# Grouping the output products of the RWKV head pairs by kind instead of by chunk

## The chip, the cores and the metric

The kernel runs on one core of a Trainium2 chip. The metric is device time in microseconds (us), from launch to the end of the program. Engines are named as in the profile: PE is TensorE (matrix products), PEld its weight loads, DVE is VectorE, ACT is ScalarE, POOL is GpSimd, SP is SyncE, which issues the transfers.

## The reference

Two blocks of a model work on 512 tokens with 1024 features. The first has two layers, each a feed-forward part, a mixer and a second feed-forward part. The mixer runs six RWKV heads, six heads of dilated attention and a convolution side by side. Each RWKV head keeps a 64x64 state and steps it over the tokens:

```
state = state * w_t + sa * b_t + v_t * k_t      # sa = state a_t
y_t   = state r_t
...
y = ((y - mean(y)) * rsqrt(var(y) + eps)) * ln_w + ln_b
out = (y + bonus) * g
```

The second block (gated linear attention, sparse attention, convolutional feed-forward parts) follows and is not touched.

## The kernel before

The two heads of a pair lie side by side: head 0 on partitions 0 to 63 (`hb[0]`), head 1 on 64 to 127 (`hb[1]`). There are three pairs a layer and two layers, six pairs in all. `rwkv_pair` cuts the 512 tokens into 8 chunks of 64. For each chunk the output is a sum of two products, collected in one bank of PSUM (`pY`, [128, 8, 64]): scores by values, `SR[h][:, n]` by `VV[h][:, n]`, with 128 rows of contraction and 64 columns; and from the second chunk on queries by the state at the chunk's start, `Rt` by `S`, with 64 rows and 64 columns. That is 16 score products and 14 state products a pair, 30 together, 180 in the program. A float32 product of this kind shows as two MATMUL records in the trace.

The states come from a loop of seven steps before (L683 on PE, L684 on DVE). Behind the output products stand a group norm (L695 to L705: sums on DVE, a square on ACT, Newton steps of `rsqrt` at L300 to L305, a product on POOL), transposes back to features by tokens (L711, copied by ACT), the gate (L715) and two DVE operations (L716, L717) that finish `out[i]`.

Order: the mixer's parts are traced by turns (`MIXER`), and a scheduler ranks them, so on each engine the instructions of the three pairs (PSUM banks `rr`, `rz`, `rx`), of the attention (banks `at`, `po`), and of `mem_kv` (bank `mm`, operands `mh`, `ml`) are interleaved. Each engine then runs its list strictly in order. `mem_kv` multiplies eight weight blocks, each in 24 MATMULs of 256 columns at L270 to L272. Then `out_proj` runs twice over eight blocks of 12 MATMULs: the first time over pairs `rr` and `rz` and the convolution, the second time over attention and pair `rx`. Each weight block is split into a high part by ACT (L258, `whi`) and a low part by DVE (L259, `wlo`), with two buffers each.

Of the kernel before, what the change touches and what calls it, by code (L numbers as in the profile page):

```python
# [18 lines left out]
T = 512  # L19
# [18 lines left out]
# ---------------------------------------------------------------- constants that depend on shapes alone  # L38

def const_pack():  # L40
    """Small tables side by side, [128, n], and where each begins."""
# [26 lines left out]
def dil_table():  # L68
    """ALiBi and pattern multiplicity of the dilated attention, [head, p, u], key minus query = u - 384 - p."""
    p = np.arange(128)[:, None]  # L70
    u = np.arange(512)[None, :]
    d = p + 384 - u
    m = (d <= 128) * 1.0 + (d % 4 == 0) + (d % 16 == 0)
    m = np.where(d >= 0, m, 0.0)
    with np.errstate(divide="ignore"):
        lm = np.log(m)
    out = [np.where(m > 0, -s * d + np.where(m > 0, lm, 0.0), NEG) for s in SLOPES_6]
    return np.ascontiguousarray(np.stack(out).astype(np.float32))
# [9 lines left out]
def nsa_table():  # L88
    """ALiBi of the causal heads, [head, p, u], u as above."""
    p = np.arange(128)[:, None]  # L90
    u = np.arange(512)[None, :]
    d = p + 384 - u
    return np.ascontiguousarray(np.stack([np.where(d >= 0, -s * d, NEG) for s in SLOPES_8]).astype(np.float32))


def cmp_tables():
    """Bias [2, p, 2, head, 32] of the tokens' tiles over compressed blocks, and which count [p, 4, 32]."""
# [9 lines left out]
def gla_masks():  # L107
    """[2, p, 512]: by levels, keys p in the first half and queries in the second half of one block."""
# [13 lines left out]
# ---------------------------------------------------------------- layout of the inputs  # L122

def pack_w(w):
    """[K, N] to [N/128, 128, K]: the 128x128 tiles of each block of 128 columns side by side."""
# [4 lines left out]
class Vecs:  # L130
    """Vectors over features as columns of 128."""
# [14 lines left out]
# ---------------------------------------------------------------- the program  # L146
# [4 lines left out]
# where the hidden units of the feed-forward parts lie  # L151
HIDDEN = ["r0"] * 8 + ["r1"] * 8 + ["aq"] * 3 + ["ap"] * 3

# the order of the mixer's parts, by turns
# [13 lines left out]
class Part:  # L168
    """A part of the program that is traced by turns, and where its tiles come from. The scheduler takes its first turn
    in the order of the program, the later ones by the part's rank from a place in the program on."""  # L170
# [16 lines left out]
class Net:  # L187
# [21 lines left out]
    def on(self, heap, bank, lane=""):  # L209
        """Where tiles come from until the next call."""  # L210
        self.heap, self.bank, self.lane = heap, bank, lane

    def drive(self, parts, plan):
        """Traces parts of the program by turns; the plan names parts, with the number of turns."""
# [5 lines left out]
    def rank(self, base, n):  # L220
        """The scheduler's rank of what is traced next, counted from a place in the program: low ones go first."""
        self.tc.cur_priority = base + RANK * n
# [17 lines left out]
    def s(self, shape, tag="s", dt=F32, heap=None):  # L240
        """A tile of at most 2 KB a partition from a heap."""
# [8 lines left out]
    # ------------------------------------------------ products of float32 in three passes  # L250

    def load_w(self, dram, cols):
        """One chunk of weights: DMA, then its high and low parts (exact: hi + lo is the weight to 24 bits)."""
# [8 lines left out]
    def gemm(self, ps, w, xs, k0, k1, first, last):  # L262
        """ps (+)= W^T X over the k-tiles k0..k1 of the chunk; xs gives (hi, lo) of a k-tile."""
# [10 lines left out]
    def proj(self, dram, xs, n=T):  # L274
        """One block of 128 outputs over 1024 inputs, left in PSUM."""
# [5 lines left out]
    def split(self, src, scale=None, heap=None):  # L281
        """(hi, lo) of a tile, times a constant; src may lie in PSUM."""
# [11 lines left out]
    # ------------------------------------------------ norms  # L294

    def rsqrt(self, x, shape, tag="rs", iters=3):
        """1/sqrt(x) of positive x by Newton's steps."""
# [10 lines left out]
    def bcast(self, r, q, heap=None, bank=None):  # L308
        """[128 tok, q] to [128, q*128], the same on every partition."""
# [11 lines left out]
    def norm_r(self, x, nt=T):  # L321
        """The tokens' 1/rms over 1024 features, the same on every partition."""
# [16 lines left out]
    def scaled(self, x, gname, l0=0, nt=T, heap=None):  # L339
        """(hi, lo) of x*g, tile by tile."""  # L340
# [10 lines left out]
    # ------------------------------------------------ feed-forward parts  # L351
# [50 lines left out]
    def out_proj(self, x, w, m, k0=0, k1=KT, bank="mm"):  # L402
        """x += W^T m over the k-tiles k0..k1; m their (hi, lo)."""
# [5 lines left out]
    def spill(self, x):  # L409
        """Parks x in DRAM; the function that it returns brings it back."""  # L410
# [14 lines left out]
    # ------------------------------------------------ helpers of the mixers  # L425

    def to_tok(self, src, to=None):
        """[128 ch, 512 tok] to [128 tok, 4, 128 ch]."""
# [9 lines left out]
    def head_sums(self, ps, c0, src):  # L438
        """Sums over each of two heads' 64 channels: ps[tok, j, c0:c0+2]."""
# [3 lines left out]
    def head_bcast(self, r, heap=None):  # L443
        """r [128 tok, 4, 2] to PSUM [128 ch, 512], each head's number over its 64 channels."""
# [7 lines left out]
    def derived(self):  # L452
        """Vectors worked out once: 1 - mu, 1 - k_a, halves of biases, the product of the heads' gains."""
# [16 lines left out]
    # ------------------------------------------------ RWKV  # L470

    def shifted(self, l, blk, win, xs, R):
        """A projection with its token shift, p + (prev - p) mu, in features by tokens."""
# [8 lines left out]
    def rwkv_shared(self, l, win, xs, R):  # L482
        """What the low-rank parts read: tanh of the decays', the rates', sigmoid of the gates'; and their weights."""
# [10 lines left out]
    def rwkv_pair(self, l, i, win, xs, R, shared, out):  # L494
        """Two heads, by chunks of 64 tokens; out gets the result in features by tokens.

        Within a chunk f_t = r_t + sum_{s<t} N[s, t] f_s is solved with D, the inverse of the diagonal blocks of 16, and
        M = (N without these) D, whose fourth power is zero: f = D (r + M (r + M (r + M r))). Rows are (head, token in
        its chunk); of head 0 the scores' rows are the keys of b, then those of k, of head 1 the other way round."""
# [9 lines left out]
        # decay, rate  # L509
# [21 lines left out]
        # keys  # L531
# [32 lines left out]
        # scores, keys by queries: a's columns before the token, r's up to it  # L564
# [13 lines left out]
        # the diagonal blocks, a block in a partition, and their inverses  # L578
# [7 lines left out]
        # tokens by channels  # L586
# [75 lines left out]
        # the state's step over a chunk: S' = ec (G^T S + H), [j, i] of each head; the first state is zero  # L662
# [23 lines left out]
        # outputs, and the norm of each head's group  # L686
        pY = self.ps([128, 8, 64])
        for n in range(8):
            for h in range(2):
                self.T.matmul(pY[hb[h], n], SR[h][:, n], VV[h][:, n], start=True, stop=True)  # L690
                if n:
                    self.T.matmul(pY[hb[h], n], Rt[hb[h], 64 * n:64 * n + 64], S[hb[h], n], start=False, stop=True, skip_group_check=True)
# [27 lines left out]
    # ------------------------------------------------ attention  # L720

    def softmax(self, ps, bias, n, z, heap=None):
        """exp(ps + bias - max) by rows; z gets the rows' sums."""
# [10 lines left out]
    def causal_pair(self, score, V, tables, z, po, heap):  # L734
        """Causal attention of two heads, four tiles of queries each: po[head's channel, t] without the division by z.
        score(ps, h, i) leaves a tile's products with the keys up to its end; V(h, b) gives a block of a head's values."""
# [32 lines left out]
    def dilated_pair(self, l, i, win, xs, R, out):  # L769
        """The dilated attention of two heads: one softmax over all keys, each as often as patterns hold it."""  # L770
# [38 lines left out]
    # ------------------------------------------------ convolution  # L809
# [82 lines left out]
    # ------------------------------------------------ attention to the memory  # L892

    def mem_kv(self, l):
        """Keys [dh, m] and values [m, dh] of the memory's four heads, to DRAM."""
# [52 lines left out]
    def mem_attend(self, heads, mq, kv, out, c0=4):  # L948
        """Some of the four heads' results, (hi, lo) by features and tokens."""
# [44 lines left out]
    # ------------------------------------------------ gated linear attention  # L994

    def gla_pair(self, i, win, xs, R, low, mk, Vk, rr, out):
        """Two heads over all tokens. A query and an earlier key share, on one level of halving, a block whose
        middle lies between them; their decay is the product of the two parts up to the middle, both at most 1."""
# [125 lines left out]
    # ------------------------------------------------ sparse attention  # L1124

    def twice(self, f, g, n=T, heap=None):
        """The high and the low parts of half of a tile, each on both halves of the partitions. Against queries whose
        parts lie on the halves, two passes give the product of float32."""
# [8 lines left out]
    def windows(self, kc, which):  # L1137
        """The compressed blocks' halves, by the parity of the token and the channel, with their positions added."""
# [11 lines left out]
    def hidden(self, ph):  # L1150
        """Hidden units of the compressed blocks, [128 units, 2, keys and values, 2 groups, 32]; the 32nd block is none."""
# [17 lines left out]
    def compressed(self, kc, vc, q, gates, C):  # L1169
        """The compressed blocks' part, to C[pair][channel of two heads, t]."""  # L1170
# [85 lines left out]
    def stream_pair(self, u, st, q, K, V, gates, O, bank):  # L1256
        """Causal attention of two heads over all tokens' keys and values, to O, the second onto the first: all blocks (eight are selected of
        eight), or the window, which holds all tokens."""
# [143 lines left out]
# ---------------------------------------------------------------- the launch  # L1402

def pack_first(a):
    """The first block's inputs as the program reads them."""
# [105 lines left out]
```

## Time and profile before

| | us |
|---|---|
| runs of the kernel: lowest, median, highest | 3510.12, 3514.63, 3515.13 |
| profiled execution: first to last instruction (span) | 3510.5 |
| PE busy in the span | 3465.2 |
| DVE, ACT, POOL busy | 1749.7, 1229.8, 538.4 |
| score products of all pairs (L690), first to last start | 661.3 to 1832.9 |

The profiled execution has only its span; the median run is 4.1 us longer. Engines work at once, so their busy times overlap. PE is busy in nearly all of the span, but a busy PE is not PE at its peak.

### The profile page before, as it was taken

The numbers are of one execution on the slowest core, as the hardware profiler recorded it, in microseconds if no ns is written. First come the engines' busy times: TensorE is split into PE (matmuls) and PEld (weight loads), VectorE is DVE, ScalarE is ACT, GpSimd is POOL, SyncE is SP. The second block draws the span as 40 slices with busy tenths as digits, with TensorE's granted clock in tenths as the row PEclk, the third lists the DMA queues.
The fourth block names the chain that finished last, engine by engine and source line by source line (L and its number), as shares of the span: only waits on it lengthen the run. The fifth ranks groups of instructions, "written<-read, shape, count | busy, mean of one in ns | idle before, by whom it ended". The sixth has DMA issues, their size and how long they took to land.

```text
span 3510.5 us, 43279 instructions
## 1 busy us (share of the span) xinstructions
PE 3465.2 (99%) x17126; PEld 2763.0 (79%) x17126; DVE 1749.7 (50%) x2857; ACT 1229.8 (35%) x1946; POOL 538.4 (15%) x509
## 2 busy tenths in 40 slices
PE   8999999999999999999999999999999999999998
PEld 6888777778888888877777888777888887778886
DVE  4433498454333443359755333385655354455532
ACT  3222334343222222233434222244433234643332
POOL 2110024011111111012401111120111000211100
PEclk9999999999999999999989999999999999999999
DMA  3223322132223222332214223321322333122232
GB/s 137 91 95 108 100 78 64 34 116 92 96 92 95 95 91 93 112 98 77 53 39 137 96 96 99 112 79 63 106 91 95 105 123 102 49 92 95 92 96 79
DMA packets 127594, 321.55 MB, mean 92 GB/s; under 512 B 32385, under 2 KB 34977, under 8 KB 127393
## 3 DMA queue, kind: packets, MB, share of 16 engines
q1 hardware_dynamic: 127392, 318.80, 28.6%
q8 instruction: 134, 2.20, 0.3%
q14 instruction: 68, 0.55, 0.1%
HBM read 303.81 MB, written 14.94 MB: 91 GB/s over the span
## 4 chain that ended last, share of the span: by engine, by line
PE 94%; DVE 3%; POOL 1%; issue 1%; ACT 0%; DMA 0%; SPq 0%; DVEq 0%; POOLq 0%; ACTq 0%
PE mm L272 13%; PE mm L270 12%; PE mm L271 12%; PE at L270 8%; PE at L271 8%; PE at L272 8%; PE rr L272 4%; PE rr L270 4%; PE rr L271 4%; PE rx L270 3%; PE rx L272 3%; PE rx L271 3%; PE po L748 1%; PE at L798 1%; POOL Z L616 1%
## 5 line engine op out<-in xcount | busy, mean ns | idle before, releaser
L258 ACT ACTIVATE whi<-raw 128x1024 fp32r<-128x1024 f32 (+2 forms) x566 | 562.1, 994 | 1680.9 <-issue 529.6
L259 DVE TENSOR_TENSOR wlo<-raw,whi 128x1024 fp32r<-128x1024 f32 (+2 forms) x566 | 651.2, 1151 | 505.8 <-ACT whi L258 491.0
L270 PE MATMUL mm<-xh,whi 128*128 128x512 f32 x1216 | 486.4, 400 | 9.7 <-ACT whi L258 9.7
L272 PE MATMUL mm<-xh,wlo 128*128 128x512 f32 x1216 | 487.8, 401 | 0.0
L271 PE MATMUL mm<-xl,whi 128*128 128x512 f32 x1216 | 485.1, 399 | 0.7 <-DVE xl L347 0.7
L270 PE MATMUL at<-xh,whi 128*128 128x512 f32 x736 | 291.7, 396 | 0.0
L272 PE MATMUL at<-xh,wlo 128*128 128x512 f32 x736 | 291.0, 395 | 0.0
L271 PE MATMUL at<-xl,whi 128*128 128x512 f32 x736 | 290.8, 395 | 0.0
L270 PEld LDWEIGHTS mm<-xh,whi 128*128 128x128 f32 x1216 | 229.3, 189 | 65.6 <-ACT whi L258 10.1
L373 POOL TENSOR_TENSOR fg<-fg,bR 128x512 f32<-128x512 f32 x88 | 155.3, 1767 | 806.5 <-ACT fg L372 806.5
L272 PEld LDWEIGHTS mm<-xh,wlo 128*128 128x128 f32 x1216 | 229.0, 188 | 61.3 <-issue 3.9
L271 PEld LDWEIGHTS mm<-xl,whi 128*128 128x128 f32 x1216 | 229.1, 188 | 57.3 <-issue 2.5
L270 PE MATMUL mm<-hi,whi 128*128 128x512 f32 x652 | 259.5, 399 | 2.4 <-ACT hi L287 1.5
L272 PE MATMUL mm<-hi,wlo 128*128 128x512 f32 x652 | 257.6, 396 | 0.0
L271 PE MATMUL mm<-lo,whi 128*128 128x512 f32 x652 | 257.4, 395 | 0.1
L331 POOL TENSOR_TENSOR nacc<-nacc,nsq 128x512 f32<-128x512 f32 x70 | 107.0, 1528 | 772.7 <-ACT nsq L330 772.2
L272 PEld LDWEIGHTS at<-xh,wlo 128*128 128x128 f32 x736 | 138.1, 188 | 36.1 <-DVE wl L514 1.5
L271 PEld LDWEIGHTS at<-xl,whi 128*128 128x128 f32 x736 | 138.2, 188 | 34.5 <-issue 1.5
L272 PE MATMUL rr<-xh,wlo 128*128 128x512 f32 x416 | 164.4, 395 | 0.8 <-DVE wlo L259 0.8
L270 PEld LDWEIGHTS at<-xh,whi 128*128 128x128 f32 x736 | 138.2, 188 | 33.8 <-ACT gy L1004 0.8
L270 PE MATMUL rr<-xh,whi 128*128 128x512 f32 x416 | 164.6, 396 | 0.0
L271 PE MATMUL rr<-xl,whi 128*128 128x512 f32 x416 | 164.3, 395 | 0.0
(667 smaller groups left out, 5975.1 us busy)
## 6 DMA issues: line engine op xcount, KB each, us to landing
raw<-ffn_gu SPq DMA_DIRECT2D x176, 512.0 KB
raw<-c_gu SPq DMA_DIRECT2D x88, 512.0 KB
raw<-ffn_dn SPq DMA_DIRECT2D x64, 448.0 KB
raw<-w_in SPq DMA_DIRECT2D x46, 512.0 KB
raw<-ffn_dn SPq DMA_DIRECT2D x32, 512.0 KB
raw<-c_dn SPq DMA_DIRECT2D x32, 448.0 KB
raw<-a_w_in SPq DMA_DIRECT2D x17, 512.0 KB
park<-x SPq DMA_DIRECT2D x32, 256.0 KB
```

The source lines that it names most:

```text
L258: self.A.activation(hi, raw, AF.Copy)
L259: self.V.tensor_tensor(lo, raw, hi.bitcast(F32), OP.subtract)
L270: self.T.matmul(ps, wh, xh, start=first and j == 0, stop=False)
L271: self.T.matmul(ps, wh, xl, start=False, stop=False)
L272: self.T.matmul(ps, wl, xh, start=False, stop=last and j == nk - 1)
L331: self.G.tensor_tensor(acc, acc, sq, OP.add)
L373: self.G.tensor_tensor(g, g, R, OP.mult)
L616: self.G.tensor_tensor(Z[:, 0, 0:t, t:16], Z[:, 0, 0:t, t:16], tmp[:, 0:t, 0:nt], OP.add)
L748: self.T.matmul(po[64 * h:64 * h + 64, i * 128:(i + 1) * 128], V(h, b), PT[h][:, b * 128:(b + 1) * 128], start=b == 0, stop=b == i)
L798: self.T.matmul(ps, q[b, i * 128:(i + 1) * 128], k[b, 0:(i + 1) * 128], start=True, stop=True)
```

## The change

All 16 score products of a pair are issued first, then all 14 state products. The first score product of each head now marks the bank as fresh (`start=n == 0`) where every score product did so before; the other products add to the bank. Operands, shapes and number of products stay. The two loops take one more line, so every line below stands one further down (L692 becomes L693, L711 becomes L712). Comments and docstrings were emptied too.

```
         pY = self.ps([128, 8, 64])
         for n in range(8):
             for h in range(2):
-                self.T.matmul(pY[hb[h], n], SR[h][:, n], VV[h][:, n], start=True, stop=True)
-                if n:
-                    self.T.matmul(pY[hb[h], n], Rt[hb[h], 64 * n:64 * n + 64], S[hb[h], n], start=False, stop=True, skip_group_check=True)
+                self.T.matmul(pY[hb[h], n], SR[h][:, n], VV[h][:, n], start=n == 0, stop=True, skip_group_check=True)
+        for n in range(1, 8):
+            for h in range(2):
+                self.T.matmul(pY[hb[h], n], Rt[hb[h], 64 * n:64 * n + 64], S[hb[h], n], start=False, stop=True, skip_group_check=True)
```

The scheduler makes a new order of it. On PE, the output products of the last pair (`rx`) of the first layer stood like this before, a score product and a state product of one head, then of the other:

```order
L690 MATMUL rx_4921<-VV_4357,SR_4271 64x64
L690 MATMUL rx_4921<-VV_4358,SR_4272 64x64
L690 MATMUL rx_4921<-VV_4357,SR_4271 64x64
L692 MATMUL rx_4921<-rS_4815,Rt_4156 64x64
L690 MATMUL rx_4921<-VV_4358,SR_4272 64x64
L692 MATMUL rx_4921<-rS_4815,Rt_4156 64x64
L690 MATMUL rx_4921<-VV_4357,SR_4271 64x64
L692 MATMUL rx_4921<-rS_4815,Rt_4156 64x64
```

Now they stand in two blocks, the heads in turns in each (the last score products and what follows them):

```order
L690 MATMUL rx_4921<-VV_4357,SR_4271 64x64
L690 MATMUL rx_4921<-VV_4358,SR_4272 64x64
L690 MATMUL rx_4921<-VV_4357,SR_4271 64x64
L690 MATMUL rx_4921<-VV_4358,SR_4272 64x64
L693 MATMUL rx_4921<-rS_4815,Rt_4156 64x64 x14
L712 MATMUL rr_4801<-cpack,gn_y_4717 64x128 x4
L938 MATMUL mm_5662<-cpack,mvf_5660 128x128 x2
```

In the first pair (`rr`) other work still cuts into the two blocks at six places, in the second (`rz`) at three.

The second place is PE at the start of `out_proj`. Before, the last `mem_kv` block is followed by its transposes (L937) and by whole blocks of `out_proj` (`mm_5817`), and the transposes of pair `rx` (L711) come 24 products later:

```order
L272 MATMUL mm_5752<-mh_5459,wlo_5749 128x256
L937 MATMUL mm_5779<-cpack,mvf_5777 128x128 x2
L270 MATMUL mm_5817<-hi_5801,whi_5820 128x512
L271 MATMUL mm_5817<-lo_5802,whi_5820 128x512
L272 MATMUL mm_5817<-hi_5801,wlo_5821 128x512
L270 MATMUL mm_5817<-hi_5805,whi_5820 128x512
```

Now the first four transposes of `rx` stand ahead of `out_proj`, the other four and the gate (L716) inside its first two blocks (`mm_5817`, `mm_5837`), which run in turns:

```order
L272 MATMUL mm_5752<-mh_5459,wlo_5749 128x256
L712 MATMUL rx_4977<-cpack,gn_y_4955 64x128 x4
L938 MATMUL mm_5779<-cpack,mvf_5777 128x128 x2
L270 MATMUL mm_5817<-hi_5801,whi_5820 128x512
L271 MATMUL mm_5817<-lo_5802,whi_5820 128x512
L272 MATMUL mm_5817<-hi_5801,wlo_5821 128x512
L270 MATMUL mm_5817<-hi_5805,whi_5820 128x512
L712 MATMUL rx_4984<-cpack,gn_y_4955 64x128 x4
L270 MATMUL mm_5837<-hi_5801,whi_5840 128x512
L271 MATMUL mm_5837<-lo_5802,whi_5840 128x512
```

The third place is DVE between the first sum of pair `rx` and the last Newton step of its `rsqrt`, 31 instructions now. It begins so:

```order
L696 TENSOR_REDUCE gn_m_4952<-rx_4921 128x8
L305 SCALAR_TENSOR_TENSOR gn_r_4882<-gn_r_t_4883,gn_r_4882 128x8
L697 TENSOR_SCALAR gn_m_4952<-gn_m_4952 128x8
L303 TENSOR_TENSOR gn_r_t_4883<-gn_r_4882 128x8
L699 TENSOR_TENSOR gn_y_4955<-rx_4921,gn_m_4952 128x512
L304 SCALAR_TENSOR_TENSOR gn_r_t_4883<-gn_r_t_4883,gn_v_4879 128x8
L717 SCALAR_TENSOR_TENSOR bv_3662<-yf_4793,vec,bv_3662 128x512
```

The Newton steps of pair `rz` (`gn_r_4882`) now lie between those of `rx`; before they were over when `rx` began. The second layer's order changes in the same way. POOL's order stays; a few transfers on SP change places.

## Rows read from the trace of the kernel before

**Rows 1.** The page: PE's busy time, and the chain that ended last, by engine.

```profile
PE 3465.2 (99%) x17126; PEld 2763.0 (79%) x17126; DVE 1749.7 (50%) x2857; ACT 1229.8 (35%) x1946; POOL 538.4 (15%) x509
...
PE 94%; DVE 3%; POOL 1%; issue 1%; ACT 0%; DMA 0%; SPq 0%; DVEq 0%; POOLq 0%; ACTq 0%
```

**Rows 2.** Chain of waits, 640 to 800 and 1780 to 1900 us: shares by line.

```profile
by line: PE mm L272 17.1%; PE mm L270 16.8%; PE mm L271 16.4%; PE at L798 3.9%; PE po L748 3.1%; PE rz L692 2.9%; PE rx L690 2.9%; PE rz L690 2.8%; PE rx L692 2.8%; PE rr L690 2.4%; PE rr L692 2.1%; PE at L742 2.1%; PE rr L272 1.2%; PE at L
by line: PE mm L272 19.0%; PE mm L270 18.6%; PE mm L271 17.9%; PE rz L692 3.9%; PE rx L690 3.7%; PE rx L692 3.7%; PE rz L690 3.7%; PE po L748 3.5%; PE rr L690 3.2%; PE rr L692 2.8%; PE at L742 2.8%; PE at L798 2.4%; PE rx L676 1.6%; PE rx L
```

**Rows 3.** Chain of waits, longest pieces: start, us taken, line and MATMUL records.

```profile
654.14 0.61 PE rx L672 x16
655.71 0.73 PE rr L676 x20
662.01 0.26 PE rr L690 x2
692.68 1.90 PE rx L676 x32
703.48 0.40 PE rx L690 x2
716.14 1.05 PE rr L715 x2
717.19 0.56 PE rz L711 x4
```

**Rows 4.** Windows cut where the granted clock is low: busy us (instructions), clock, DMA.

```profile
668.59:672.00 3.41, 3.41 (x35) 2.85 (x35) 0.63 (x5) 0.99 (x4) 0.00 (x0) 0.50 0.00 0
682.25:695.90 13.65, 13.65 (x91) 10.65 (x92) 4.43 (x15) 1.23 (x2) 0.00 (x0) 0.50 0.09 34
702.73:712.97 10.24, 10.24 (x50) 8.44 (x51) 2.71 (x5) 2.57 (x5) 0.00 (x0) 0.50 0.01 2
1808.65:1822.30 13.65, 13.65 (x91) 10.78 (x92) 4.79 (x19) 1.23 (x2) 0.00 (x0) 0.50 0.08 31
1829.13:1835.95 6.82, 6.82 (x35) 5.42 (x35) 1.56 (x3) 0.75 (x2) 0.00 (x0) 0.50 0.00 0
```

**Rows 5.** Chain of waits in the last four of these windows: shares by line.

```profile
by line: PE rz L692 25.2%; PE rz L690 23.9%; PE rx L676 13.9%; PE mm L272 8.4%; PE mm L270 8.4%; PE at L449 7.7%; PE mm L271 6.2%; PE po L748 3.7%; PE rx L683 3.0%
by line: PE rx L692 23.7%; PE rx L690 23.2%; PE rr L711 18.0%; PE mm L272 10.4%; PE rz L711 8.3%; PE mm L270 8.3%; PE mm L271 8.3%
by line: PE rz L692 24.9%; PE rz L690 21.4%; PE rx L676 13.9%; PE mm L270 10.0%; PE mm L272 10.0%; PE at L449 7.7%; PE mm L271 6.2%; PE po L748 3.7%; PE rx L683 3.0%
by line: PE rx L692 35.5%; PE rx L690 30.4%; PE rr L711 14.5%; PE mm L272 9.3%; PE mm L270 6.2%; PE mm L271 6.2%
```

**Rows 6.** Timeline of PE, first layer, end of `mem_kv`: start, us, instruction [idle before].

```profile
708.73 0.41 PE L271 MATMUL mm<-ml,whi 128*128 128x256 f32 x1
708.94 0.41 PE L272 MATMUL mm<-mh,wlo 128*128 128x256 f32 x1
...
713.01 0.37 PE L270 MATMUL mm<-mh,whi 128*128 128x256 f32 x1
...
716.07 1.12 PE L715 MATMUL rr<-lora_u,lora_w 64*128 64x512 f32 x2
...
725.76 0.41 PE L937 MATMUL mm<-cpack,mvf 128*128 128x128 f32 x2 [0.61 <-ACT whi L258]
```

**Rows 7.** Timeline of DVE in the same stretch: start, us, instruction [idle before].

```profile
707.55 0.69 DVE L695 TENSOR_REDUCE gn_m<-rx 128x8 f32<-128x512 f32 x1 [6.09 <-PE rx L692]
...
717.89 1.22 DVE L259 TENSOR_TENSOR wlo<-raw,whi 128x1024 fp32r<-128x1024 f32 x1
...
723.14 0.17 DVE L304 SCALAR_TENSOR_TENSOR gn_r_t<-gn_r_t,gn_v 128x8 f32<-128x8 f32 x1
...
729.00 0.69 DVE L407 TENSOR_TENSOR x<-mm,x 128x512 f32<-128x512 f32 x1 [2.11 <-PE mm L272]
```

**Rows 8.** Timeline of POOL: the product that ends the group norm of pair `rx`.

```profile
726.45 1.34 POOL L705 TENSOR_TENSOR gn_y<-gn_y,gn_r 128x512 f32<-128x512 f32 x1 [23.78 <-DVE gn_r L305]
```

## Prediction

> **What bounds the kernel now.** I read the page first: PE is busy for 99% of the span, and 94% of the chain that ended last lies on PE [rows 1]. So the question for any change is whether it takes time from PE, and whether PE then has to wait for something that it has hidden so far. Next I asked the chain of waits for the two stretches in which the output products run, the end of the mixer in each layer. In 640 to 800 us the six shares at L690 and L692 (pairs rr, rz, rx) add up to 15.9% of 160 us, 25.4 us; in 1780 to 1900 us they add up to 21.0% of 120 us, 25.2 us [rows 2]. Together 50.6 us for 180 products, 0.28 us each, and all of it lies on the chain. Elsewhere in the program nothing of the change is executed.
>
> The third view is the list of pieces of that chain [rows 3]. A group of two records is one product. In turns by kind, one takes 0.26 us at the full clock (662.01) and 0.40 us at the low one (703.48). Work of the same shape that stands in one kind costs much less. L672 is a product of 128 rows by 64 columns into the same kind of bank, the heads in turns, added to later by state products, which is the shape of a score product: 16 records take 0.61 us, 0.076 us a product. L676 has the shape of a state product, 64 by 64: 20 records take 0.73 us, 0.073 us a product. So about 0.18 us of the 0.26 us is not arithmetic; it appears when a product of 128 rows and one of 64 rows alternate, and when the two heads do not follow each other within one kind.
>
> The fourth view is the granted clock. [...] The chain in the four long ones gives the output products 49.1% of 13.65, 46.9% of 10.24, 46.3% of 13.65 and 65.9% of 6.82 us, 22.3 us in sum [rows 5]; at these lines the chain spends more than anywhere else in each. Other work takes the remaining 25.5 us of the 47.8.
>
> **What the change removes.** A pair's 30 products stand in two blocks now. Priced by the neighbours of like shape at the full clock, 180 x 0.076 = 13.7 us. Work of other shapes still cuts in at nine places in a layer, and each of the three pairs changes from one kind to the other once. For each of these 12 I take 0.1 us, between nothing and the 0.18 us above, since much of the other work that cuts in has the shape of one of the two kinds: 2.4 us for both layers. That is 16.1 us against 50.6: **34.5 us saved**. Bounds: at the low clock the like work costs 1.90 us for 32 records (692.68), 0.119 us a product, so 21.4 + 2.4 us, and only 27 us are saved; with no cost at the cuts 37 us.
>
> [...] Score products of both heads use all 128 rows; only their columns differ. In the row the 16 records of L672 do follow each other in 0.61 us [rows 3]. [...]
>
> **The clock.** The low level comes in stretches in which products in turns are the largest item [rows 5]. The stretch before them, with blocks of L672 and L676 at 654 to 656 us, has small products too and runs at the full rate by its own prices [rows 3]. I therefore take it that the low level goes where the turns go. The products' share of this is in the 34.5 us already. For the other 25.5 us: a memory product takes 0.21 us in the low stretch (708.73 to 708.94), and 24 take 3.06 us at the full clock (713.01 to 716.07), 0.128 us each [rows 6]. So 25.5 x (1 - 0.128 / 0.21) = **10.0 us saved**. Bounds: nothing, if the low stretches stay, and 12.8 us if all of it halves.
>
> [...]
>
> **What it adds: waits at the end of the mixer.** Before, PE was so slow that everything else was early: its wait at the last transposes was 0.61 us [rows 6]. Now PE comes to `out_proj` some 20 us sooner in each layer, but VectorE has the same work to do. Two places matter.
>
> First, the transposes of pair rx (L712) stand ahead of `out_proj` now, where they stood two blocks later. PE's queue can't pass them, and they need the group norm of rx. DVE's queue from the first sum to the last Newton step has 31 instructions: 17 small ones at 0.17 us, 13 of at most 0.69 us, one split of a weight block of 1.22 us [rows 7], 13.1 us, and then POOL's product, 1.34 us [rows 8]: 14.4 us. PE meanwhile has three memory blocks of 3.06 us [rows 6], three groups of four transposes at about 0.56 us and two gates at 1.05 us [rows 3], 13.0 us. PE waits about 1.4 us, and everything in `out_proj` behind it.
>
> Second, the first two blocks of `out_proj` run in turns and end together. So the next two weight blocks are split only after both: two additions into x and a split, three DVE instructions of 0.69 us [rows 7], about 2.1 us, of which four products of PE cover about 1.0. Another 1.1 us. Together 2.5 us a layer, **5 us lost**. Bounds: nothing, if the handoffs overlap better than this, and 10 us a layer, if DVE's queue is held up at each of its own waits for PE and ACT, as the 6.09 and 2.11 us idle times in its rows now are [rows 7]. Transfers are no candidate: in the low windows the sixteen DMA engines are busy for 0.09 of the time or less [rows 4].
>
> **Sum.** -34.5 - 10.0 + 5 = -39.5 us, against the profiled span of 3510.5 us 3471.0. The median of the runs is 4.1 us above this span, and I keep that distance: 3514.6 - 39.5 = **3475 us**.
>
> **The rivals.**
> *The clock stays low* (chance 0.14): the low level is a matter of small products and not of turns. For: the low windows hold L676 too. Against: the stretch at 654 us. Then 27 + 0 - 2.5 (PE is slower, so less waiting) = 24.5 us, 3490.
> *No new waits* (0.13): 44.5 us, 3470.
> *DVE's queue binds* (0.14): waits of 10 us a layer, 24.5 us, 3490. For: in the 31 instructions rz's Newton steps now lie between those of rx. Against: of the 20.2 us that the same chain takes now (707.55 to the end of POOL's product at 727.79), 3 us and more are idle.
> *Score products don't pair* (0.04): 39.5 - 17 = 22.5 us, 3492.
> *The change doesn't do what it says* (0.02): the 0.18 us belongs to adding into a bank just written, not to the alternation. For: the added state product follows its own score product now. Against: L683's loop adds in the same way. Then nothing is saved, 3515.
> *Slower* (0.02): the last chain stands alone. If the transposes ahead of `out_proj` had to wait out the whole norm of rx, 20.2 us a layer, and the two blocks in turns were held up by 5 us more by their second transposes, that were 50 us against 44.5 saved: 3520. It decides from 22 us of wait a layer; the 13 us of PE work between speak against it.
>
> **How the numbers follow.** The forecast has 0.51, and its own range is 3468 to 3483. The range for 8 in 10 has to take in the clock and the queue cases: 3462 to 3492; below 3462 both savings would have to be at their upper bound with no wait, 37 + 12.8 = 49.8 us. About 0.2%, 7 us, can be told from no change. Faster by more than that holds in all cases but the last two: 0.95; within it 0.03; slower 0.02.
>
> **What would show it.** In the profile after: records at L690 in blocks with about 0.04 us each, and the shares of L690 and L693 in the two stretches at 7 to 9 us a layer instead of 25; a granted clock of 1.00 where four windows read 0.50; a wait of PE before the first transposes of rx (L712) and at the third block of `out_proj`, of one to three us each, ended by POOL, DVE or ACT. I would be wrong if the records at L690 stayed at 0.1 us and more, if the low windows stayed, or if PE's idle time at the start of `out_proj` came to 10 us a layer.

## The result and the profile after

| | before | changed |
|---|---|---|
| first comparison, median of 4 runs each | 3512.38 us | 3476.44 us (3467.64 to 3479.94) |
| ratio, 95% interval | | 0.9895 (0.9875 to 0.9914) |
| second comparison, median of 13 and 6 runs | 3514.46 us | 3469.75 us (3465.07 to 3471.21) |
| ratio, 95% interval | | 0.9862 (0.9836 to 0.9889) |
| profiled span | 3510.5 us | 3464.6 us |

The change makes the kernel faster by 35.9 us in the one comparison and 44.7 us in the other. The forecast was 3475 us, 39.5 us less.

The page of the changed kernel, engines and the chain that ended last; it answers to [rows 1]:

```profile
PE 3419.1 (99%) x17126; PEld 2729.0 (79%) x17126; DVE 1748.7 (50%) x2857; ACT 1232.1 (36%) x1946; POOL 538.8 (16%) x509
...
PE 94%; DVE 3%; POOL 1%; DMA 1%; issue 1%; ACT 0%; SPq 0%; DVEq 0%; POOLq 0%; ACTq 0%
```

PE is busy for 46.1 us less with the same 17126 records, about what the span lost (45.9 us). So the time came out of PE's work and not out of its waits.

The chain of waits of the changed kernel, pieces of the output products in the first layer (start, us taken, line and records; state products are L693 now); it answers to the pieces at L690 in [rows 3]:

```profile
662.60 0.61 PE rr L690 x14
...
673.07 0.85 PE rz L690 x24
...
675.10 0.61 PE rz L693 x16
...
683.96 1.08 PE rx L690 x32
685.04 0.96 PE rx L693 x28
```

A pair's 16 score products (32 records) take 1.08 us and its 14 state products 0.96 us, 0.068 us a product, where two records alone took 0.26 us before. Blocks cut by other work cost somewhat more: 24 records in 0.85, 16 in 0.61 us.

The windows of the changed kernel, end of the mixer, first layer (busy us and instructions of PE, PEld, DVE, ACT and POOL, then granted clock, DMA share and GB/s); they answer to [rows 4]:

```profile
655.00:670.00 15.00, 15.00 (x204) 11.52 (x200) 5.08 (x19) 4.36 (x13) 0.00 (x0) 1.00 0.08 29
670.00:690.00 20.00, 20.00 (x269) 17.78 (x268) 16.86 (x50) 8.07 (x15) 3.10 (x2) 1.00 0.23 74
690.00:705.00 15.00, 14.21 (x89) 11.03 (x88) 11.94 (x28) 9.43 (x21) 1.04 (x1) 1.00 0.39 120
705.00:720.00 15.00, 14.59 (x60) 10.61 (x59) 7.71 (x12) 3.69 (x6) 0.00 (x0) 1.00 0.52 170
```

The granted clock is 1.00 throughout, also in the second layer's end, where [rows 4] read 0.50 for 47.8 us. PE is no longer busy for all of the last two windows: these are its waits.

Where the time went: compare the k-th record of PE in both traces. The changed kernel is 1.0 us ahead at 640 us of the kernel before, 24.7 us from 760 us on, 24.8 at 1780, 45.9 from 1900 us to the end. All of the gain, 23.7 + 21.1 = 44.8 us, lies in the ends of the two mixers. The repeat gives 23.7 + 21.1 again. Outside them the executions differ by a few short stretches at 0.50 that come in every kernel here at changing places (the profiled executions' mean granted clocks are 0.985 to 0.996; 28.6 us of low clock in this profile, half of it at the very end; 38.9 in the repeat's), and this moves the time by some us (the two profiled spans are 3464.6 and 3468.0 us). So in the following each kernel is judged by its gain in the two mixers' ends, beside its ratio.

A second sum is used below: over all records of the output products, the time from a record's start to the start of the next record on PE. Before it is 51.0 us in both layers together (the chain gave 50.6), now 15.8 us.

### The profile page after: what moved, and what is told of

The parts are those of the page before. It is cut to its first block, busy times and chain, and to the rows that moved or that the text cites. A ratio compares the mean times of both kernels' runs of the same rounds, so it can differ in the third digit from the quotient of the medians.

```text
span 3464.6 us, 43276 instructions
## 1 busy us (share of the span) xinstructions
PE 3419.1 (99%) x17126; PEld 2729.0 (79%) x17126; DVE 1748.7 (50%) x2857; ACT 1232.1 (36%) x1946; POOL 538.8 (16%) x509
## 4 chain that ended last, share of the span: by engine, by line
PE 94%; DVE 3%; POOL 1%; DMA 1%; issue 1%; ACT 0%; SPq 0%; DVEq 0%; POOLq 0%; ACTq 0%
PE mm L272 13%; PE mm L270 13%; PE mm L271 13%; PE at L271 8%; PE at L270 8%; PE at L272 8%; PE rr L272 4%; PE rr L271 4%; PE rr L270 4%; PE rx L272 3%; PE rx L270 3%; PE rx L271 3%; PE po L749 1%; PE at L799 1%; PE at L743 1%
## 5 line engine op out<-in xcount | busy, mean ns | idle before, releaser
L270 PE MATMUL mm<-xh,whi 128*128 128x512 f32 x1216 | 485.1, 399 | 9.1 <-ACT whi L258 9.0
L270 PE MATMUL at<-xh,whi 128*128 128x512 f32 x736 | 291.1, 395 | 0.0
L270 PEld LDWEIGHTS mm<-xh,whi 128*128 128x128 f32 x1216 | 228.9, 188 | 65.1 <-ACT whi L258 9.5
L270 PE MATMUL mm<-hi,whi 128*128 128x512 f32 x652 | 259.8, 400 | 3.3 <-ACT hi L287 1.5
L270 PEld LDWEIGHTS at<-xh,whi 128*128 128x128 f32 x736 | 138.2, 188 | 34.1 <-ACT gy L1005 0.8
L270 PE MATMUL rr<-xh,whi 128*128 128x512 f32 x416 | 164.2, 395 | 0.0
```

Of the source, the lines that this page charges most:

```text
L270: self.T.matmul(ps, wh, xh, start=first and j == 0, stop=False)
```

## The experiments

The theory: what cost 0.18 us a product was the change of kind, from a product of 128 rows to one of 64 rows or back. Rivals: it was that the two heads did not alternate within a kind; or it was adding to a region of PSUM that had just been written. For the clock: the low level goes with the turns; or with small products as such. For the waits: DVE's queue has cover left; or it is about to bind. The edits are shown against the changed kernel.

**The changed kernel again** (no edit).

> The changed kernel once more, nothing else. My theory (the cost was the change between products of 128 rows and of 64 rows, and it is gone) expects the records of L690 and L693 at 16 us in both layers together as in its first profile (8.3 + 7.5), a granted clock of 1.00 in both ends of the mixer, and a time 1.0 to 1.3% below the kernel before. The rival that the full clock in these two places was luck of one execution expects at least one stretch of 0.50 there.

Measured: 15.8 us for the products (8.3 + 7.5), clock 1.00 in both ends, 44.8 us gained there; the ratio is in the table above. As the theory expects.

**By chunk, but the heads together.**

```diff
 for n in range(8):
     for h in range(2):
         self.T.matmul(pY[hb[h], n], SR[h][:, n], ...)
-for n in range(1, 8):
-    for h in range(2):
+    for h in range(2 if n else 0):
         self.T.matmul(pY[hb[h], n], Rt[hb[h], 64 * n:64 * n + 64], ...)
```

> By chunk as before, but within a chunk both heads' score products and then both heads' state products, so half as many changes of kind. If the change of kind is what costs (0.15 us at each, 0.06 us for two records of like kind that follow, 0.1 us for the first two after a change), a chunk takes 0.27 + 0.26 us, that is 0.13 us a product, 24 us for 180 and some 1 to 3 more for other work between; the whole then lies about 26 us below the kernel before for the products, less whatever clock it gives back. If only the alternation of heads mattered, the products would cost as little as in the changed kernel, 16 us. If adding to a bank just written were the cost, they would stay at about 47 to 51 us, since each state product still follows its own score product closely. On the clock I have two theories: turns bring the low level (then some stretches at 0.50 come back in the mixers' ends), or only the share of time lost in them (then none).

Measured: 3479.68 us, ratio 0.9894 (0.9866 to 0.9923). Products 24.6 us. The chain of this kernel, pair rx of the first layer (state products are L692):

```profile
688.25 0.27 PE rx L690 x4
688.51 0.26 PE rx L692 x4
688.77 0.27 PE rx L690 x4
689.04 0.26 PE rx L692 x4
```

Four records, two products, now cost what one product cost in turns. The state products still follow their own score products directly, so adding to a region just written is not the cost. The clock stays at 1.00 in both ends: half the changes did not bring the low level.

**The two kinds in blocks, one head after the other.**

```diff
-for n in range(8):
-    for h in range(2):
+for h in range(2):
+    for n in range(8):
         self.T.matmul(pY[hb[h], n], SR[h][:, n], ...)
-for n in range(1, 8):
-    for h in range(2):
+for h in range(2):
+    for n in range(1, 8):
         self.T.matmul(pY[hb[h], n], Rt[hb[h], 64 * n:64 * n + 64], ...)
```

> The kinds in two blocks as in the changed kernel, but in each block all of head 0 and then all of head 1. If the change of kind costs and the heads' alternation only adds, a record takes 0.058 us (single records at the ends of the changed kernel's blocks do), 360 of them 21 us, with the changes and cuts 23 to 25 us. If the alternation of heads is the main thing, each record costs the 0.106 us that the second record of a product took in turns: 38 us and 2 to 4 for the changes. [...]

Measured: 3477.79 us, ratio 0.9888 (0.9861 to 0.9915). Products 22.6 us. Timeline of PE, pair rx of the first layer:

```profile
686.70 1.90 PE L690 MATMUL rx<-VV,SR 128*64 128x64 f32 x32
```

32 records in 1.90 us, 0.058 us from start to start, against 1.08 us with the heads in turns. So the alternation of heads is worth 6.8 us (22.6 less 15.8) of the 35.2, and the rest, 28.4 us, is the change of kind together with the clock under it: an estimate from [rows 3] and [rows 5], 22.3 x (1 - 0.26 / 0.40), puts the low clock's part of it at 8 us. Both kinds gain from the alternation: score products cost 12.7 us here and 8.3 in the changed kernel, state products 10.0 and 7.5. The 0.106 us of a second record in turns was not the price of a head without its partner but of the second record behind a change: behind the first one here it also is 0.107 us, and then 0.058.

**In turns, but each state product four products late.**

```diff
-for n in range(8):
-    for h in range(2):
+order = [(n, h) for n in range(8) for h in range(2)]
+for j in range(20):
+    if j < 16:
+        n, h = order[j]
         self.T.matmul(pY[hb[h], n], SR[h][:, n], ...)
-for n in range(1, 8):
-    for h in range(2):
+    if j >= 6:
+        n, h = order[j - 4]
         self.T.matmul(pY[hb[h], n], Rt[hb[h], 64 * n:64 * n + 64], ...)
```

> The kinds in turns as before, but each state product adds to the region that was written four products earlier, not to the one just written (the first six score products of a pair come first, then ten of each kind in turns, then the last four state products). If the change of kind costs, 20 products of a pair cost 0.26 to 0.28 us and 10 cost 0.08 us: 36 to 39 us in all, and stretches at 0.50 come back. If adding to a region just written were the cost, it is gone: 16 to 18 us as in the changed kernel.

Measured: 3495.21 us, ratio 0.9941 (0.9917 to 0.9965). Products 35.7 us. The chain of this kernel (L692 are score, L695 state products):

```profile
693.20 0.61 PE rx L692 x14
693.81 0.25 PE rx L695 x2
694.06 0.26 PE rx L692 x2
694.32 0.25 PE rx L695 x2
```

and its windows cut where the clock is low:

```profile
670.50:673.91 3.41, 3.41 (x35) 2.85 (x37) 0.67 (x5) 0.99 (x4) 0.00 (x0) 0.50 0.00 0
697.80:704.63 6.83, 6.83 (x41) 6.05 (x40) 2.58 (x6) 2.41 (x5) 1.04 (x1) 0.50 0.01 2
1786.66:1800.31 13.65, 13.65 (x93) 10.60 (x93) 3.47 (x11) 2.32 (x8) 0.00 (x0) 0.50 0.00 0
```

A turn costs 0.25 to 0.26 us though nothing is added to a region just written; that rival falls a second time. The new `start=n == 0` is not the cause either: these turns have it and cost what the old ones cost. With the turns the low level is back, for 23.9 us.

The kernels so far beside each other; changes of kind are counted between neighbouring records of the output products in the trace of both layers, low clock in the mixers' ends:

| kernel | changes of kind | products, us | at 0.50, us | gain in the mixers' ends, us |
|---|---|---|---|---|
| before | 142 | 51.0 | 47.8 | |
| in turns, late | 102 | 35.7 | 23.9 | 17.8 |
| by chunk, heads together | 72 | 24.6 | 0 | 35.2 |
| blocks, heads apart | 6 | 22.6 | 0 | 36.3 |
| changed | 6 | 15.8 | 0 | 44.8 |

**The blocks twice, and turns ahead of the blocks.** Both repeat work whose result is written over.

```diff
+... the whole of the two loops of the changed kernel once more (first kernel),
+... or the loop of the kernel before, in turns (second kernel)
 for n in range(8):
     for h in range(2):
         self.T.matmul(pY[hb[h], n], SR[h][:, n], ...)
```

> The output products of a pair are made twice, both times in two blocks as in the changed kernel; the second time writes the same numbers over the first. It asks whether many small products bring the low clock by themselves. My theory (turns bring it) expects a granted clock of 1.00 in the mixers' ends, and twice 15.8 us for the products plus two changes of kind more in each pair (12 x 0.15 = 1.8 us): 33 to 35 us for the four blocks, the whole some 18 to 20 us above the changed kernel. If small products as such bring the low level, stretches at 0.50 appear there, and with twice 16 us of small products at up to 0.119 us each and other work beside them the whole lies 30 us or more above the changed kernel.

> The output products of a pair are made twice: first in turns as in the kernel before, then in two blocks as in the changed kernel, over the first. My theory expects the turns to cost again what they cost before (47 to 51 us for 180), the blocks behind them 16 to 18 us, and stretches at 0.50 of some 30 to 50 us together in the mixers' ends: the whole 16 to 20 us above the kernel before, 60 us above the changed one. If the low level in the kernel before was not tied to the turns, the clock stays at 1.00 and the whole is only some 46 us above the changed kernel.

Measured, blocks twice: 3488.85 us, ratio 0.9931 (0.9912 to 0.995), 19.1 us above the repeat of the changed kernel (22.3 us if each is taken against the kernel before that ran beside it). The four blocks take 29.1 us, less than the 33 to 35 expected. Turns and blocks: 3541.02 us, ratio 1.0084 (1.006 to 1.0108), 71 us above it (74.5 us in the same way); the turns take 53.2 us, the blocks 19.4 us. Windows of the first kernel and then of the second:

```profile
655.00:690.00 35.00, 33.20 (x571) 28.72 (x569) 15.53 (x39) 9.96 (x22) 0.00 (x0) 1.00 0.10 32
690.00:693.40 3.40, 3.40 (x19) 3.40 (x18) 2.58 (x28) 0.37 (x1) 0.00 (x0) 0.50 0.39 119
1751.54:1754.95 3.41, 3.41 (x22) 3.06 (x21) 2.68 (x15) 0.68 (x3) 0.00 (x0) 0.50 0.00 0
1770.00:1826.60 56.60, 53.81 (x694) 44.94 (x692) 32.17 (x95) 23.97 (x53) 4.03 (x3) 1.00 0.20 64
1826.63:1830.04 3.41, 3.25 (x8) 2.58 (x9) 2.51 (x5) 1.21 (x3) 0.00 (x0) 0.50 0.95 263
```

```profile
678.34:691.99 13.65, 13.65 (x130) 10.64 (x131) 1.65 (x3) 0.60 (x1) 0.00 (x0) 0.50 0.01 1
695.41:705.65 10.24, 10.24 (x99) 8.15 (x99) 0.00 (x0) 0.00 (x0) 0.00 (x0) 0.50 0.01 2
1777.43:1780.84 3.41, 3.41 (x23) 3.07 (x21) 2.33 (x13) 0.38 (x1) 0.00 (x0) 0.50 0.01 3
1797.91:1814.98 17.07, 17.07 (x108) 11.59 (x106) 1.92 (x8) 1.90 (x4) 0.00 (x0) 0.50 0.00 1
1825.22:1838.87 13.65, 13.65 (x98) 9.77 (x100) 1.12 (x2) 1.32 (x4) 0.00 (x0) 0.50 0.01 1
1845.70:1852.53 6.83, 6.83 (x90) 5.90 (x91) 0.00 (x0) 0.00 (x0) 0.00 (x0) 0.50 0.01 2
sum 64.85, PE 64.85 PEld 49.13 DVE 7.03 ACT 4.20 POOL 0.00; mean PE 10.81 PEld 8.19 DVE 1.17 ACT 0.70 POOL 0.00
```

Twice as many small products in blocks leave 35 and 57 us of the mixers' ends at 1.00; two short stretches at 0.50 (6.8 us) came, right behind waits of PE (1.80 us at 689.45, 0.99 and 0.25 us before 1826.79) and with no output product in them. A third, at 1751.54, lies ahead of the second layer's output products (they begin at 1767.7) and behind no wait, but just behind 16 products of only two columns:

```profile
1749.26 1.95 PE L441 MATMUL at<-cpack,asq 128*128 128x2 f32 x16
```

The same work with turns ahead has 64.9 us at 0.50, in six windows, and PE is busy for every microsecond of them. The window at 1777.43 also lies ahead of its output products (from 1793.9), at the same work as the one at 1751.54; the other five, 61.4 us, lie where the turns are. So in the output products the low level goes with the turns and not with the number of small products. Ahead of them it also came with neither turns nor a wait, and not every time: in the changed kernel nothing at 0.50 follows the same 16 products. The second kernel's expectation was 10 us short; more of the time was at 0.50 than I had allowed (30 to 50 us).

**Nine Newton steps in the group norm.**

```diff
-        rs = self.rsqrt(vs, [128, 8], "gn_r")
+        rs = self.rsqrt(vs, [128, 8], "gn_r", iters=9)
```

> The changed kernel with nine Newton steps in place of three in the group norm of each pair: 18 more small DVE instructions, at 0.17 us about 3.1 us more in each pair's chain, and 9.2 us more of DVE a layer. It asks how near DVE's queue is to binding, since the waits that I forecast hardly came. In the profile of the changed kernel POOL's product for rx ends 0.8 us before PE comes to the transposes of rx. So my theory expects a wait of PE there of about 2.3 us, and up to 2 us more at the first splits of out_proj, 2 to 5 us a layer, 4 to 10 us in all. If DVE's queue as a whole were the bound, all 9.2 us a layer would show, 18 us. If there were far more cover than that profile shows, nothing.

Measured: 3481.76 us, ratio 0.991 (0.9894 to 0.9926). Against the changed kernel's profile 4.9 and 5.5 us are lost in the mixers' ends. PE's waits of 600 to 780 us and of 1740 to 1920 us (us in total, times, longest; the first line is ahead of the output products and also in the kernel before):

```profile
PE rx L637 <- DVE ZD L634: 2.1, 1, 2.1
PE rz L716 <- ACT yf L714: 1.5, 1, 1.5
PE mm L938 <- DVE gn_r_t L303: 0.9, 1, 0.9
PE mm L938 <- DVE gn_r L305: 0.6, 1, 0.6
...
PE rz L716 <- ACT yf L714: 1.5, 1, 1.5
PE mm L938 <- DVE gn_r_t L303: 0.9, 1, 0.9
PE mm L271 <- DVE lo L288: 0.8, 1, 0.8
PE mm L270 <- ACT hi L287: 0.7, 1, 0.7
PE mm L938 <- DVE gn_r L305: 0.4, 1, 0.4
```

3.0 and 4.3 us of waits a layer, where the changed kernel has 1.2 (below): 4.9 us more in all of the 18 us that were added to DVE. The other 5.5 us lie beside two stretches at 0.50 (708.60 to 715.43 and 1824.76 to 1828.17 us) that the changed kernel did not have there. Each begins at the end of a wait of PE or right behind it (1.47 us until 708.80; 0.67 and 0.85 us before 1824.02), as two in the kernel with the blocks twice did. Not every such wait brings one: the kernel with turns ahead of the blocks waits 1.81 us at 716.11, and none follows. The size is as expected, the place is not: the order on PE came out otherwise, the transposes of rx stand behind the first products of out_proj there, and PE waits for rz instead. DVE's queue as a whole does not bind.

**The 64-row products for G and R together, then those for H.**

```diff
 G = self.s([128, 8, 64], "G")
 self.V.tensor_tensor(G, pG, ...)
-pH = ...  (loop at L672)
 pR = ...  (loop at L676)
 self.V.tensor_tensor(Rt, ...)
+pH = ...  (loop at L672)
```

> The changed kernel with the same idea one step earlier: the 64-row products for G and for R stand together, then the 128-row products for H, so that a pair has one change of kind less on each side of H. If a change of kind costs 0.15 us, 12 changes less are worth 1.8 us at most, less where other work cuts in anyway: no difference that the times can tell (within 0.2%), and L666, R and H together some 1 to 2 us less than the 23.2 us of the changed kernel in the trace. If more hangs on it (R is ready earlier, H later, so the first state step waits), a wait of PE at the state steps appears.

Measured: 3486.28 us, ratio 0.9921 (0.9906 to 0.9936): not the same but some 12 us worse than the changed kernel's profile in the mixers' ends (11.6 us from the record at which the two orders on PE part to the one at which they meet again). A miss. By the sum from start to start G, R and H cost 25.9 us, not less than the changed kernel's 23.2, since other work cuts into them at new places; the output products cost 12.8 us, 3.0 less. PE's waits, second layer, 1740 to 1860 us:

```profile
PE mm L938 <- DVE mvf L935: 3.9, 2, 2.5
PE mm L270 <- ACT hi L287: 1.3, 1, 1.3
PE mm L270 <- DVE x L407: 0.4, 1, 0.4
```

5.6 us here and 3.6 in the first layer, against 1.2 and 1.2. H comes later, so the state steps do, and rz's outputs stand at 688 to 692 us beside those of rx, no longer at 673 to 676: the norms of two pairs fall together at the end of the mixer. That is 6.8 us of the 12. The rest I have not settled; two stretches at 0.50 (6.8 us together) are part of it, again right behind waits of PE, of 0.98 us at 712.80 and 2.54 us at 1804.77. No version here beats the changed kernel.

## Why the prediction was right, and where its sizes were off

**The products** (forecast -34.5 us, measured -35.2). The change of kind is the cost: the step was right, and the price from L672 and L676 (0.076 us a product, [rows 3]) held, 0.068 in undisturbed blocks. The sum with the cuts was forecast at 16.1 us and is 15.8. That it fits so well is partly luck: at 0.068 us the 180 products are 12.2 us and not 13.7, so the cuts and the changes cost 3.6 us and not 2.4. At the full clock a record followed by one of the other kind is followed 0.148 to 0.152 us later; two records of one kind start 7 and then 51 ns apart if the heads take turns. What PE does in the longer time at a change was not shown.

**The rival that score products don't pair.** It fell: the 32 records of rx at L690 take 1.08 us, against 0.96 us for 28 at L693. Score products use all 128 rows in both heads, and with the heads in turns they still run at 1.08 us in place of the 1.90 with the heads apart. No run shows the 17 us that the rival's sum takes off (96 x 0.18); the runs showed 8.3 us for all 96 score products in the changed kernel.

**The clock** (forecast -10.0 us). The 25.5 us of other work in the forecast are the five windows of [rows 4], 47.8 us, less the products' share of the last four by [rows 5], 22.3 us. Of the 44.8 us gained, 35.2 are the products and PE waits 1.2 us more, so 10.8 us are left for other work, which now runs at 1.00. This is a remainder and not measured by itself, but three kernels support it: by chunk with heads together 8.8 us of its 35.2 are not the products', blocks with heads apart 7.9 of 36.3 (10.0 and 10.8 with the waits that each added), and in turns but late, where half of the low time stayed, 2.5 of 17.8. That the low level comes with turns while PE counts as busy throughout is shown by the kernel with turns ahead: 61.4 us at 0.50 in five windows, PE busy in all of it. Other stretches at 0.50 lie at or behind waits of PE: with the blocks twice (1.80 us, and 0.99 with 0.25), nine Newton steps (1.47, and 0.67 with 0.85), and G and R together (0.98 and 2.54). In the turns of the kernel before the profile counts a record for 0.22 to 0.37 us and the next one starts at most 0.25 us later, so its busy time can't show whether the engine stood still in between. Why the turns bring the low level stays open.

**The waits** (forecast +5 us, measured +1.2): the term that was mis-sized, and the main reason why the gain in the trace is 45 and not 39.5 us. In the trace it came out as the rival *No new waits* (0.13) said: 44.5 us. PE's waits in the changed kernel, 600 to 780 us, the same in the second layer but for the first line:

```profile
PE rx L637 <- DVE ZD L634: 2.1, 1, 2.1
PE mm L938 <- DVE gn_r_t L304: 0.6, 1, 0.6
PE mm L270 <- DVE x L407: 0.4, 1, 0.4
PE mm L938 <- ACT whi L258: 0.2, 1, 0.2
```

1.2 us a layer, of which 0.6 were there before at the same place in the code. The first forecast wait, 1.4 us ahead of the transposes of rx, does not exist. Timelines of DVE, POOL and PE show why:

```profile
686.20 0.68 DVE L696 TENSOR_REDUCE gn_m<-rx 128x8 f32<-128x512 f32 x1
...
687.12 0.69 DVE L699 TENSOR_TENSOR gn_y<-rx,gn_m 128x512 f32<-128x512 f32 x1
687.73 0.16 DVE L304 SCALAR_TENSOR_TENSOR gn_r_t<-gn_r_t,gn_v 128x8 f32<-128x8 f32 x1
...
697.58 0.17 DVE L305 SCALAR_TENSOR_TENSOR gn_r<-gn_r_t,gn_r 128x8 f32<-128x8 f32 x1
697.92 1.04 POOL L706 TENSOR_TENSOR gn_y<-gn_y,gn_r 128x512 f32<-128x512 f32 x1 [8.08 <-DVE gn_r L305]
699.77 0.60 PE L712 MATMUL rx<-cpack,gn_y 128*64 128x128 f32 x4
```

DVE is through in 11.55 us and not 13.1: I had added durations, but an instruction of 0.69 us is followed 0.61 us later by the next. POOL's product takes 1.04 us, not the 1.34 of [rows 8]. It ends at 698.96, and PE comes to L712 only at 699.77, after 13.8 us, of which 13.2 are its own work (forecast 13.0) and 0.6 the wait in the second row above. So 1.4 us of wait became 0.8 us of cover. The second wait, at the third block of out_proj, came, at 0.41 us in place of 1.1: in the row PE waits at L270 for an addition into x (L407), the release that was forecast. The kernel with nine Newton steps shows how thin the cover is: with 3.1 us more in each chain the waits grew by 1.8 and 3.1 us a layer.

**The sum.** With the measured terms it is -35.2 - 10.8 + 1.2 = -44.8 us; since the 10.8 are the remainder, the terms fit of themselves, but the total is measured. That is what both profiles of the changed kernel show, and what the second comparison's medians show (-44.7). The first comparison's median, 1.4 us from the forecast, was close partly by luck: the waits were forecast 3.8 us too high, and three of its four runs had a mean granted clock of 0.992 to 0.993 against 0.996 in the profiled one.

## What to carry to other kernels

Small products cost by their neighbours here: 0.26 us a product in turns of 128 and 64 rows, 0.068 us in undisturbed blocks. So group them by shape first, and within a shape let the two heads take turns (0.034 us a record, against 0.058 for one head alone); a row of like-kind neighbours in the trace gave the price beforehand (0.076 us a product). Count the changes of shape in the order that the engine gets, since a scheduler's other work makes changes too, and an edit that saves a few by moving whole steps can lose more than it saves: with G and R together the output products cost 3.0 us less and the mixers' ends took some 12 us more. When adding up a queue of short instructions, add start to start (11.55 us for DVE's queue here) and not durations (13.1).

## What was not expected of the hardware

Records of one head alone take 0.058 us, against 0.034 with the heads in turns; most of the old cost was the change of shape, 0.15 us, and then 0.1 us for the second record behind it. In the turns the low clock came while PE counted as busy for all of 61.4 us. It also came at or behind waits of only 1 to 2.5 us, so that a wait can cost more than its length: with nine Newton steps 5.5 us were lost beside two such stretches, besides the 4.9 us of the waits themselves. And behind a DVE instruction of 128 by 512, 0.69 us long, the next one starts 0.08 us before it ends (687.12 and 687.73 in the changed kernel).
